# Products of an identity put ahead of the score products of a hybrid of four mixers

## The chip, the cores and the metric

The kernel runs on one core of one Trainium2 chip. The metric is the device time of one execution in microseconds. The engines are named as in the profile: PE is TensorE, DVE is VectorE, ACT is ScalarE, POOL is GpSimd, SP is SyncE.

## The reference

T = 256 positions, D = 1024, two layers, all in float32. Each layer projects h with w_in, gives a quarter of the result to each of four mixers, joins their outputs with w_out and normalises; then comes a feed-forward part, dense in layer 0, a mixture of 8 experts (top 2) in layer 1.

```python
for l in range(DEPTH):
    p = jnp.einsum('btd,dc->btc', h, w_in[l])
    pa, pb, pc, pd = _split(p, MIXER_COLS)
    ya = _hgrn2_mixer(pa, lb_all[l], hgrn_norm_g[l])
    yb = _gla_mixer(pb, gla_gate_w2[l], gla_gate_b[l], gla_norm_g[l])
    yc, v_first = _rwkv7_mixer(pc, v_first, v_mix, ...)
    yd = _retnet_mixer(pd, positions, log_gamma)
    mix = jnp.einsum('btc,cd->btd', jnp.concatenate([ya, yb, yc, yd], -1), w_out[l])
    h = _layer_norm(DN_ALPHA * h + mix, ln1_g[l], ln1_b[l])
    f = _swiglu(h, ...) if l % 2 == 0 else _moe(h, ...)
    h = _layer_norm(DN_ALPHA * h + f, ln2_g[l], ln2_b[l])
```

HGRN2 and GLA are the same recurrence, `out = q decay-weighted over the past (k, v)`: `scores = einsum('bhik,bhjk,bhijk->bhij', q, k, decay)`, `out = scores v + (q exp(cum)) state`. The mixer's output is normalised per head, multiplied by a gate and goes to w_out.

## The kernel before

Every float32 product of a weight matrix is done as three products of a rounded half H and a rest L (`wH` by ACT, line 133, `wL` by DVE, line 136; helper `mm` at 146 issues each matmul, `tr` at 149 each transposition). Their results are named `Pws_ps` and `Pas_ps` (projections by w_in, in two forms), `bank_acc` and `bank_r` (the products of w_out, whose left side is the mixers' outputs `YT`, and of the residual, `h` by `alphaI`). The four projections of a mixer are cut into jobs whose steps can be issued between other work: `between(n)` issues n steps of the pending jobs and then lets the body follow the last of them. The order on each engine is then set by the scheduler of the language from dependences and its own costs, so that it differs from the order of the code.

A layer's mixers run in the order RWKV, RetNet, HGRN2, GLA. RWKV walks over chunks (`Prw_po` is a chunk's output product, `rw_OC` the collected outputs); `head_norm` normalises per head, with the rsqrt (`hn_rs<-rs_ve,mhalf`) on POOL; the last step is the transposition of `rw_OC` into `Prw_ps14`, 16 pairs of 64x64 products. RetNet (`rt_o`) is normalised by the same helper.

HGRN2's scores (`hgrn_scores`) are formed for each half of the heads a and each of two heads s: decays by products with `c_hlR` (`Phs_ps`, `Phs_psd`), their exponentials `hg_E`, then nine small products over 64 partitions into the banks p1 and p2 (`Phs_p1p`), which the profile counts as 18. Two sets of them are 36. `Ppo_ps` are the output products by the scores (`lin_S`). GLA's (`gla_scores`) are alike: `gs_E`, two products per head into `Pgs_ps`, `Ppo_ps`; its gate products are `Pga_ps`. The normalised outputs of HGRN2 and GLA (`y_late`) are transposed late, inside w_out's loop (`LATE = (0, 2)`, `self.tails`, run from `down`), by four transpositions `Ppy_ps` each.

PSUM is in three pools: 3 banks for accumulation ("acc"), 2 for RWKV ("r") and 3 for the others ("o"). A helper `keep_warm(n)` multiplies the identity `eyeR` by itself (128 x 512 columns) n times into a bank of its own that nobody reads; it is used in a few places, among them between the two late transpositions of layer 0 (four products) and in the layer norms.

Of the kernel before, what the change touches and what calls it, by code (L numbers as in the profile page):

```python
# [44 lines left out]
TAIL, DT = 4, 4  # L45

WARM_NORM, WARM_LAST, WARM_ROUTE = 12, 4, 8

WARM_WAIT = 7

# [74 lines left out]
class Build:  # L125
# [88 lines left out]
    def keep_warm(self, n):  # L214

        b = self.acc()
        for _ in range(n):
            self.mm(b, self.eyeR, self.eyeR[:, None, :].to_broadcast([128, 4, 128]), True, True)


    def load(self, w, parts, cuts=1):
# [390 lines left out]
        self.rstd(rs, s2, eps, p)  # L612
        self.tt(o, o, rs[:, :, None].to_broadcast([128, n, 64]), OP.mult)

    def put_y(self, y, ct):

        ps = self.mx("Ppy_ps1")
        for a in range(2):
            for tt in range(2):
                self.tr(ps[:, a * 256 + tt * 128:a * 256 + tt * 128 + 128], y[:, tt, a * 128:(a + 1) * 128], self.ident)  # L620
        self.put_yt(ps, ct)
# [6 lines left out]
    def mixers(self, l):  # L628
        nc, I, c, p = self.nc, self.I, self.c, self.otp
        W = I["w_in"][l]  # L630
        self.mp, self.side, self.hp = self.rp, "r", HP
        ws = lambda c0: self.ws_steps(W, [(c0, c0 + 256)])
        as_ = lambda c0: self.as_steps(W, [(c0, c0 + 256)])
        self.jobs = []
# [92 lines left out]
    def gated_norm(self, o, g, G, ct):  # L727

        ng = self.bcast(self.t2([128, 64], n="gn_ng"), g)
        self.ts(ng, ng, 0.5, None, OP.mult, eng=self.nc.gpsimd)  # L730
        v = o.rearrange("p t (h v) -> p (t h) v", v=64)
        gv = G.rearrange("p t (h v) -> p (t h) v", v=64)
        self.tt(gv, gv, ng[:, None, :].to_broadcast([128, 8, 64]), OP.mult, self.nc.gpsimd)
        self.head_norm(v, 1e-6, False, "gn")
        if ct in LATE:
            o = self.lp.tile([128, 2, 256], F32, name="y_late")
        self.tt(o.rearrange("p t (h v) -> p (t h) v", v=64), v, gv, OP.mult)
        if ct in LATE:
            self.tails[ct] = lambda: self.put_y(o, ct)
        else:  # L740
            self.put_y(o, ct)

# [17 lines left out]
    def hgrn_scores(self, l, qT, kT, lf, V, o):  # L760
# [7 lines left out]
        for a in range(2):  # L768
# [31 lines left out]
            for s in range(2):  # L800
                r = slice(64 * s, 64 * s + 64)
                p1, p2 = self.mx("Phs_p1p21"), self.mx("Phs_p1p21")
                with self.between(FH):
                    for t in range(2):
                        self.mm(p1[:, t * 128:(t + 1) * 128], KD[r, t], QD[r, t], True, True)
                        self.mm(p1[:, 256 + t * 128:384 + t * 128], L16[r, t], L16[r, t], True, True)
                        self.mm(p2[:, t * 128:(t + 1) * 128], L32[r, t], L32[r, t], True, True)
                        self.mm(p2[0:64, 256 + t * 64:320 + t * 64], L64[r, t, 0:64], L64[r, t, 64:128], True, True)
                    self.mm(p2[:, 384:512], E[r, 0], E[r, 8], True, True)
# [12 lines left out]
    def gla_scores(self, l, qk, lf, V, o):  # L822
# [20 lines left out]
        for h in range(4):  # L843
            r = slice(32 * h, 32 * h + 32)
            ps = self.mx("Pgs_ps2")
            with self.between(FG):
                self.mm(ps[:, 0:256], E[r, 0, 0:128], E[r, 1, :], True, True)
                self.mm(ps[:, 256:384], E[r, 0, 128:256], E[r, 1, 128:256], True, True)
            d = ps.rearrange("p (t x) -> p t x", t=2)[:, :, 0:128]
# [127 lines left out]
    def rwkv(self, l, glr):  # L977
# [27 lines left out]
        self.stt(lwL, lw, 1.0, lwH.bitcast(F32), OP.add, OP.subtract)  # L1005

        A = self.t2([128, 2, T], n="rw_A")
        ps = self.mx("Prw_ps2").rearrange("p (a t) -> p a t", a=2)
        for a in range(2):
            self.mm(ps[:, a, :], a2[64:128, a * 128:(a + 1) * 128], lr[64:128, 0, :], True, True)  # L1010
        for a in range(2):
# [266 lines left out]
        ov = OC.rearrange("p c a v -> p (c a) v")  # L1278
        self.head_norm(ov, 64e-5, True, "rw")
        ps = self.mx("Prw_ps14")  # L1280
        for ch in range(4):
            for a in range(2):
                for s in range(2):
                    P, Q = slice(64 * s, 64 * s + 64), slice(64 - 64 * s, 128 - 64 * s)
                    self.mm(ps[P, a * 256 + ch * 64:a * 256 + ch * 64 + 64], OC[Q, ch, a, :], self.ident[Q, Q], True, True)
# [398 lines left out]
```

## Time and profile before

| what | us |
|---|---|
| median of three runs | 1094.89 (1093.45 to 1101.36) |
| profiled execution | 1099.03 |
| its span | 1097.2 |
| PE busy in it | 1040.8 |
| DVE busy | 789.8 |
| ACT busy | 616.8 |
| POOL busy | 60.5 |

The span is the time from the first instruction to the last; the execution's time lies a little above it. PEclk in a row is the clock that TensorE was granted, 1.00 being full speed (2.4 GHz), 0.50 the lower of its two levels (1.2 GHz). The mean granted clock of the profiled execution is 0.965.

In a row of the timeline, the first number is the start, the second the time that the group took, "x18" how many instructions it holds, and the bracket the idle time before it and who ended it.

### The profile page before, as it was taken

The page shows a single profiled execution, that of the slowest core. Times are in us where ns is not written, and L with a number is a line of the kernel's source. Part 1 is how long each engine was busy: PE and PEld are TensorE (multiplying, and loading weights), DVE is VectorE, ACT ScalarE, POOL GpSimd, SP SyncE. Part 2 cuts the span into 40 slices and gives each one's busy share as a digit, 9 for nine tenths or more (in the row PEclk, how much of TensorE's full clock was granted, in tenths as well). Part 3 has the DMA queues.
Part 4 walks back from the last instruction along what each step waited for, and adds up shares of the span by engine and source line. Part 5 has one row for each costly group of instructions (what it writes and reads, how often), then busy time and mean ns, then how long its engine had stood idle before and what let it go on. Part 6 is the DMA issues. An engine that isn't in the chain of part 4 may idle for free. (4 is left out here: it accounts for less than half of the span.)

```text
span 1097.2 us, 16969 instructions
## 1 busy us (share of the span) xinstructions
PE 1040.8 (95%) x6635; PEld 905.2 (83%) x6635; DVE 789.8 (72%) x1174; ACT 616.8 (56%) x872; POOL 60.5 (6%) x89
## 2 busy tenths in 40 slices
PE   7799989999999999899989989999999999999994
PEld 6788878789999788788877668888888888878883
DVE  4585674565556356675675578998999899989986
ACT  4634264435555342633264536787788678777862
POOL 2000021100000002000011210000000000010001
PEclk9899987999999999899988998999999999999997
DMA  9344144326666454244142095998899889979942
GB/s 299 99 119 128 57 154 155 116 78 192 193 192 228 157 192 156 87 115 131 65 164 78 12 366 191 359 381 302 313 348 362 307 306 364 357 269 328 365 179 80
DMA packets 142161, 228.83 MB, mean 209 GB/s; under 512 B 17604, under 2 KB 89848, under 8 KB 142072
## 3 DMA queue, kind: packets, MB, share of 16 engines
q1 hardware_dynamic: 135104, 219.76, 59.0%
q10 hardware_dynamic: 6968, 7.90, 2.2%
q8 instruction: 54, 0.88, 0.3%
q14 instruction: 35, 0.29, 0.1%
HBM read 224.50 MB, written 3.15 MB: 207 GB/s over the span
## 5 line engine op out<-in xcount | busy, mean ns | idle before, releaser
L136 DVE TENSOR_TENSOR wL<-raw,wH 128x1024 fp32r<-128x1024 f32 (+2 forms) x480 | 504.1, 1064 | 159.2 <-ACT wH L133 152.3
L133 ACT ACTIVATE wH<-raw 128x1024 fp32r<-128x1024 f32 (+2 forms) x481 | 441.9, 927 | 271.0 <-PE Pws_ps L146 95.8
L146 PE MATMUL Pws_ps<-XT,wH 128*128 128x256 f32 (+1 forms) x1248 | 233.2, 287 | 9.1 <-DVE rc_x L143 8.3
L146 PE MATMUL Pms_ps<-wH,e_X 128*128 128x512 f32 (+1 forms) x768 | 227.3, 374 | 0.0
L146 PEld LDWEIGHTS Pws_ps<-XT,wH 128*128 128x128 f32 (+1 forms) x1248 | 195.7, 191 | 12.8 <-DVE rc_x L143 9.2
L146 PE MATMUL Pws_ps<-XT,wL 128*128 128x256 f32 (+1 forms) x624 | 177.9, 286 | 0.0
L146 PEld LDWEIGHTS Pms_ps<-wH,e_X 128*128 128x128 f32 x768 | 142.3, 188 | 20.8
L146 PE MATMUL Pms_ps<-wL,e_X 128*128 128x512 f32 (+1 forms) x384 | 144.7, 377 | 1.0 <-DVE wL L136 1.0
L146 PEld LDWEIGHTS Pws_ps<-XT,wL 128*128 128x128 f32 (+1 forms) x624 | 119.3, 191 | 0.8 <-issue 0.3
L146 PE MATMUL bank_dn<-wH,e_aT 128*128 128x512 f32 x352 | 112.3, 396 | 0.6 <-DVE e_X L136 0.6
L146 PE MATMUL Pas_ps<-wH,XT 128*128 128x256 f32 x448 | 97.3, 305 | 4.6 <-ACT p_v L133 3.2
L146 PEld LDWEIGHTS Pas_ps<-wH,XT 128*128 128x128 f32 x448 | 76.8, 203 | 10.2 <-ACT p_v L133 4.5
L146 PEld LDWEIGHTS Pms_ps<-wL,e_X 128*128 128x128 f32 x384 | 72.2, 188 | 12.7 <-DVE wL L136 2.3
L146 PEld LDWEIGHTS bank_dn<-wH,e_aT 128*128 128x128 f32 x352 | 66.0, 188 | 16.7 <-DVE e_X L136 1.7
L146 PE MATMUL bank_dn<-wL,e_aT 128*128 128x512 f32 x176 | 69.4, 395 | 0.0
L146 PE MATMUL Pas_ps<-wL,XT 128*128 128x256 f32 x224 | 68.2, 305 | 0.5 <-DVE wL L136 0.5
L146 PEld LDWEIGHTS Pas_ps<-wL,XT 128*128 128x128 f32 x224 | 45.4, 203 | 3.1 <-DVE wL L136 1.8
L146 PEld LDWEIGHTS bank_dn<-wL,e_aT 128*128 128x128 f32 x176 | 33.1, 188 | 7.4
L146 PE MATMUL bank_acc<-wH,ffn_a 128*128 128x512 f32 x88 | 33.5, 394 | 0.0
L146 PE MATMUL bank_r<-wH,ffn_a 128*128 128x512 f32 x88 | 33.3, 392 | 0.0
L146 PE MATMUL bank_acc<-wH,YT 128*128 128x512 f32 x64 | 24.5, 416 | 1.2 <-ACT YT L133 1.2
L133 ACT ACT_TABLE_LOAD x19 | 24.4, 1283 | 1.6 <-PEq L1671 1.2
(386 smaller groups left out, 1223.8 us busy)
## 6 DMA issues: line engine op xcount, KB each, us to landing
raw<-in_moe_w_down SPq DMA_DIRECT2D x40, 1024.0 KB
raw<-in_moe_w_gate SPq DMA_DIRECT2D x32, 1024.0 KB
raw<-in_moe_w_up SPq DMA_DIRECT2D x32, 1024.0 KB
raw<-in_w_in SPq DMA_DIRECT2D x29, 1024.0 KB
raw<-in_moe_w_gate SPq DMA_DIRECT2D x16, 768.0 KB
raw<-in_moe_w_up SPq DMA_DIRECT2D x16, 768.0 KB
raw<-in_ffn_w_gate SPq DMA_DIRECT2D x11, 1024.0 KB
raw<-in_ffn_w_up SPq DMA_DIRECT2D x11, 1024.0 KB
```

Source lines behind the costliest of these rows:

```text
L133: return self.nc.scalar.activation(out=out, in_=in_, func=func, **k)
L136: return (eng or self.nc.vector).tensor_tensor(out=out, in0=a, in1=b, op=op)
L146: return self.nc.tensor.matmul(out=out, lhsT=lhsT, rhs=rhs, start=start, stop=stop)
```

## The change

A new method `fill(bank, n)` does what `keep_warm` does, but into a bank that it is given: the one that the real products right behind it in the code write. It is called in five places: 5 products ahead of RWKV's A product (layer 0 alone), 3 ahead of each of the eight score sets of HGRN2 (both layers, 24), 2 ahead of each head's scores of GLA (both layers, 16), 12 ahead of RWKV's last transposition (layer 1 alone) and 6 ahead of GLA's late transposition (layer 1 alone): 63 in all. Their values are overwritten.

```diff
+WARM_H, WARM_G, WARM_RW, WARM_LATE = 3, 2, 12, 6
...
+    def fill(self, bank, n):
+
+        for _ in range(n):
+            self.mm(bank, self.eyeR, self.eyeR[:, None, :].to_broadcast([128, 4, 128]), True, True)
...
-    def put_y(self, y, ct):
+    def put_y(self, y, ct, warm=0):
 
         ps = self.mx("Ppy_ps1")
+        self.fill(ps, warm)
...
+        self.later_layer = l > 0
...
-            self.tails[ct] = lambda: self.put_y(o, ct)
+            self.tails[ct] = lambda: self.put_y(o, ct, WARM_LATE if ct == LATE[-1] and self.later_layer else 0)
...
                 with self.between(FH):
+                    self.fill(p1, WARM_H)
                     for t in range(2):
...
             with self.between(FG):
+                self.fill(ps, WARM_G)
                 self.mm(ps[:, 0:256], E[r, 0, 0:128], E[r, 1, :], True, True)
...
-        ps = self.mx("Prw_ps2").rearrange("p (a t) -> p a t", a=2)
+        ps = self.mx("Prw_ps2")
+        self.fill(ps, 5 if l == 0 else 0)
+        ps = ps.rearrange("p (a t) -> p a t", a=2)
...
         ps = self.mx("Prw_ps14")
+        if l:
+            self.fill(ps, WARM_RW)
```

The helpers move by two lines, so `mm` is line 148 and `tr` line 151 in the changed kernel. Where the new products land is the scheduler's choice. Three places on PE follow, a row being instructions of one kind, with what they wait for.

HGRN2's scores of layer 0, first half of the heads: the end of the set s = 0 and the start of s = 1 on PE, before:

```order
L146 MATMUL Phs_p1p_1616<-hg_E 128x128
L146 MATMUL Phs_p1p_1616<-hg_E 64x64
L146 MATMUL Phs_p1p_1616<-hg_E 128x128 [waits Pool_49]
L146 MATMUL Phs_p1p_1683<-hg_E 128x128 [waits PE_49]
L146 MATMUL Phs_p1p_1683<-hg_E 128x128 x2
L146 MATMUL Phs_p1p_1684<-hg_E 128x128 [waits DVE_49,PE_49]
L146 MATMUL Phs_p1p_1684<-hg_E 64x64
```

and now:

```order
L148 MATMUL Phs_p1p_1621<-hg_E 128x128
L148 MATMUL Phs_p1p_1621<-hg_E 64x64
L148 MATMUL Phs_p1p_1621<-hg_E 128x128 [waits Pool_49]
L148 MATMUL Phs_p1p_1691<-eyeR 128x512 [waits PE_49]
L148 MATMUL Phs_p1p_1691<-eyeR 128x512 x2
L148 MATMUL Phs_p1p_1691<-hg_E 128x128 x2
L148 MATMUL Phs_p1p_1692<-hg_E 128x128 [waits DVE_49,PE_49]
L148 MATMUL Phs_p1p_1692<-hg_E 64x64
```

Three products on `eyeR` stand between the two sets, which had followed each other. Those of the set s = 0 stand six projection groups further ahead.

The end of RWKV in layer 1 on PE; `Pas_ps` are projections of a later mixer. Before, ahead of the transposition of `rw_OC` (41 more products of `Pas_ps` stand in a row above the first):

```order
L146 MATMUL Pas_ps_5885<-wH,XT 128x256 x2
L146 MATMUL Pas_ps_5885<-wL,XT 128x256
L146 MATMUL Pas_ps_5885<-wH,XT 128x256
L146 MATMUL Prw_ps_5683<-ident,rw_OC 64x64 [waits DVE_49,PE_49]
L146 MATMUL Prw_ps_5683<-ident,rw_OC 64x64 x15
L149 MATMUL Ppy_ps_5771<-ident,rt_o 128x128 [waits DVE_49]
L149 MATMUL Ppy_ps_5771<-ident,rt_o 128x128 x3
```

and now:

```order
L148 MATMUL Prw_po_5687<-rw_UV,rw_S 64x64 [waits DVE_49]
L148 MATMUL Prw_po_5687<-rw_UV,rw_S 64x64 x2
L148 MATMUL Prw_ps_5708<-eyeR 128x512 [waits PE_49]
L148 MATMUL Prw_ps_5708<-eyeR 128x512 x11
L148 MATMUL Prt_ps_5783<-p_v,rt_S_5759 128x64
L148 MATMUL Pas_ps_5640<-wH,XT 128x256
L148 MATMUL Pas_ps_5640<-wL,XT 128x256
...
L148 MATMUL Pas_ps_5641<-wH,XT 128x256
L148 MATMUL Prw_ps_5708<-ident,rw_OC 64x64 [waits DVE_49]
L148 MATMUL Prw_ps_5708<-ident,rw_OC 64x64 x15
L148 MATMUL Pas_ps_5922<-wH,XT 128x256 [waits Activation_49]
```

The 12 products stand behind the state products, and 25 products lie between them and the transposition. Seven of the 15 groups of three projection products that stood ahead of the transposition now stand behind it.

The two late transpositions of layer 1 on PE, HGRN2's first, GLA's second. Before:

```order
L146 MATMUL bank_r<-wH,YT 128x512
L149 MATMUL Ppy_ps_6486<-ident,y_late 128x128 [waits PE_49]
L149 MATMUL Ppy_ps_6486<-ident,y_late 128x128 x3
L146 MATMUL bank_acc<-wH,YT 128x512 [waits Activation_49]
L146 MATMUL bank_acc<-wL,YT 128x512
...
L146 MATMUL bank_r<-wH,YT 128x512
L146 MATMUL bank_r<-wL,YT 128x512
L149 MATMUL Ppy_ps_6503<-ident,y_late 128x128 [waits DVE_49]
L149 MATMUL Ppy_ps_6503<-ident,y_late 128x128 x3
L146 MATMUL bank_acc<-wH,YT 128x512 [waits DVE_49]
```

and now:

```order
L148 MATMUL bank_r<-wH,YT 128x512
L151 MATMUL Ppy_ps_6543<-ident,y_late 128x128 [waits PE_49]
L151 MATMUL Ppy_ps_6543<-ident,y_late 128x128 x3
L148 MATMUL Ppy_ps_6560<-eyeR 128x512 [waits PE_49]
L148 MATMUL Ppy_ps_6560<-eyeR 128x512 x5
L151 MATMUL Ppy_ps_6560<-ident,y_late 128x128 [waits DVE_49]
L151 MATMUL Ppy_ps_6560<-ident,y_late 128x128 x3
L148 MATMUL bank_acc<-wH,YT 128x512 [waits Activation_49]
L148 MATMUL bank_acc<-wL,YT 128x512
```

The new products stand ahead of the wait for GLA's `y_late`, and the eight w_out products that stood there now follow GLA's transposition.

## Rows read from the trace of the kernel before

**Rows 1.** the page: busy time and share of each engine, instructions

```profile
PE 1040.8 (95%) x6635; PEld 905.2 (83%) x6635; DVE 789.8 (72%) x1174; ACT 616.8 (56%) x872; POOL 60.5 (6%) x89
```

**Rows 2.** stretches: us; PE, PEld, DVE, ACT, POOL busy; PEclk; DMA share; GB/s

```profile
151.20:154.10 2.90, 2.90 (x23) 2.52 (x24) 1.77 (x6) 0.02 (x1) 0.00 (x0) 1.00 1.04 424
154.20:161.00 6.80, 6.80 (x26) 5.51 (x25) 3.31 (x7) 3.57 (x9) 0.46 (x1) 0.50 0.22 87
167.90:171.20 3.30, 3.30 (x17) 3.30 (x17) 0.37 (x2) 0.93 (x3) 0.00 (x0) 0.50 0.98 343
174.70:184.90 10.20, 10.20 (x47) 9.86 (x47) 4.05 (x5) 5.26 (x11) 3.62 (x3) 0.50 0.10 12
...
553.60:560.30 6.70, 6.20 (x52) 6.11 (x53) 3.92 (x8) 1.64 (x4) 0.00 (x0) 0.50 0.26 69
594.60:608.10 13.50, 13.50 (x51) 11.04 (x51) 3.31 (x7) 5.58 (x17) 3.81 (x4) 0.50 0.19 76
560.00:575.00 15.00, 15.00 (x118) 14.28 (x118) 12.87 (x22) 9.68 (x18) 0.00 (x0) 0.99 0.74 260
```

**Rows 3.** PE's timeline, layer 0, HGRN2's scores to GLA: start, us, instruction

```profile
151.21 6.33 PE L146 MATMUL Phs_p1p<-hg_E 64*128 64x128 f32 x36 [0.21 <-DVE hg_E L136]
...
168.27 0.63 PE L146 MATMUL Pas_ps<-wH,XT 128*128 128x256 f32 x2
...
168.91 0.63 PE L146 MATMUL Pas_ps<-wH,XT 128*128 128x256 f32 x2
...
175.75 3.51 PE L146 MATMUL Ppo_ps<-p_v,lin_S 128*128 128x64 f32 x16
...
185.19 0.40 PE L146 MATMUL Pas_ps<-wH,XT 128*128 128x256 f32 x2
...
185.55 0.40 PE L146 MATMUL Pas_ps<-wH,XT 128*128 128x256 f32 x2
```

**Rows 4.** timeline, end of RWKV: PE in both layers, layer 1's VectorE, GpSimd

```profile
138.85 1.15 PE L146 MATMUL Prw_ps<-ident,rw_OC 64*64 64x64 f32 x32 [1.36 <-DVE rw_OC L136]
...
554.10 1.97 PE L146 MATMUL Prw_ps<-ident,rw_OC 64*64 64x64 f32 x32 [4.45 <-DVE rw_OC L136]
...
544.83 0.69 DVE L605 TENSOR_REDUCE hn_s<-rt_o 128x8 f32<-128x512 f32 x1 [0.17 <-ACT rt_o L133]
...
546.22 0.69 DVE L136 TENSOR_TENSOR rt_o<-rt_o,hn_s 128x512 f32<-128x512 f32 x1
...
553.26 0.69 DVE L136 TENSOR_TENSOR rw_OC<-rw_OC,hn_rs 128x512 f32<-128x512 f32 x1 [0.93 <-POOL hn_rs L136]
...
549.94 3.29 POOL L136 TENSOR_TENSOR hn_rs<-rs_ve,mhalf 128x8 f32<-128x8 f32 x2 [60.11 <-DVE rs_ve L140]
```

**Rows 5.** PE's timeline, layer 1, HGRN2's scores and outputs, GLA's outputs

```profile
581.37 4.93 PE L146 MATMUL Phs_p1p<-hg_E 64*128 64x128 f32 x36
...
591.49 6.34 PE L146 MATMUL Phs_p1p<-hg_E 64*128 64x128 f32 x36 [0.87 <-DVE hg_E L136]
...
598.35 5.22 PE L146 MATMUL Ppo_ps<-p_v,lin_S 128*128 128x64 f32 x24
...
622.50 2.89 PE L146 MATMUL Ppo_ps<-p_v,lin_S 128*128 128x64 f32 x24
```

**Rows 6.** PE's timeline, layer 0: RWKV's A product, and existing products on eyeR

```profile
28.57 1.13 PE L146 MATMUL Prw_ps<-rc_x,rw_a 64*128 64x256 f32 x4 [1.32 <-DMA rw_a<-in_rwkv_a]
...
212.01 1.18 PE L146 MATMUL bank_acc<-eyeR 128*128 128x512 f32 x4
...
228.23 2.12 PE L146 MATMUL bank_acc<-eyeR 128*128 128x512 f32 x8
```

**Rows 7.** PE's timeline, layer 1: waits at GLA's scores and in out_proj

```profile
621.65 0.92 PE L146 MATMUL Pgs_ps<-gs_E 32*128 32x256 f32 x4 [0.55 <-ACT lin_S L133]
...
628.71 0.50 PE L146 MATMUL bank_acc<-wH,YT 128*128 128x512 f32 x1 [1.20 <-ACT YT L133]
...
633.08 0.66 PE L149 MATMUL Ppy_ps<-ident,y_late 128*128 128x128 f32 x4 [2.27 <-DVE y_late L136]
```

## The prediction

> **What bounds the kernel now.** I read the page first. TensorE (PE) is busy for 1040.8 of 1097.2 us [rows 1], so nearly every microsecond taken from PE's stream, or put into it, should show at the end unless it lies in one of PE's waits. The slices of granted clock say where else time hides: the profiled run's mean clock is 0.965. So the second view was the table by stretches, cut where the clock changes. It shows TensorE at 0.50, that is 1.2 GHz and not 2.4, from 154.2 to 161.0, 167.9 to 171.2, 174.7 to 184.9, 553.6 to 560.3 and 594.6 to 608.1 us, PE being busy all or nearly all of that time [rows 2]. The third view, PE's timeline, tells what PE did before: in layer 0 and again in layer 1 it ran HGRN2's scores, products of 64 partitions [rows 3, 5]; only ahead of 553.6 was it idle, 4.45 us, for rw_OC [rows 4]. I count 40.5 us at the low level in these five places; there are more elsewhere in the program that no new product touches, and I leave those as they are.
>
> The sum is made against the profiled run, 1099.03 us with a span of 1097.2; the median of the runs shown is 1094.89. I take the saving in microseconds from the one and subtract it from the other.
>
> **What a new product costs.** The kernel has the same product already: four of them take 1.18 us, eight take 2.12 [rows 6]. That is 0.30 and 0.27 us each with their start-up, and (2.12 - 1.18) / 4 = 0.24 for each further one. I take 0.24, since PE comes to them without a gap, and 0.30 as the upper bound. 63 of them are 15.1 us (up to 18.9) of PE time. What matters is how much falls into waits.
>
> **RWKV's A product, 5 products, 1.2 us: nothing.** They stand directly ahead of a product that waits 1.32 us for a DMA [rows 6]. If that load came sooner they would cost up to 1.2 us.
>
> **HGRN2 in layer 0, 12 products, 2.9 us paid.** PE is full there, so all of it is paid. What a full clock would give back, from rows at both levels: the 36 score products at 151.21 take 6.33 us, and the same 36 in layer 1 at full clock 4.93 [rows 3, 5], so 1.4. From their end at 157.5 to 161.0 there are 3.5 us of other products; a group of three projection products has a pitch of 0.64 us at the low level and 0.36 at the high one [rows 3], so 44% of such time is lost: 1.5. The stretch at 167.9 is such groups alone: 3.3 x 0.44 = 1.5. From 174.7 to 184.9, 16 output products in 3.51 us [rows 3], against 24 in 2.89 at full clock [rows 5]: 16 x (0.219 - 0.120) = 1.6; the other 6.7 us x 0.44 = 2.9. Together 8.9 us. The new products stand ahead of the scores: a score set no longer follows another directly, as the order shows. The first two stretches, 1.4 + 1.5 + 1.5 = 4.4, I count whole. Of the third, 4.5, I take two thirds, 3.0: it set in among the output products that follow the scores, and these get nothing put ahead of them. Bounds for it: 0 and 4.5. Net 7.4 - 2.9 = +4.5.
>
> **GLA in layer 0, 8 products, 1.9 us.** In the new order they replace seven residual and w_out products that stood ahead of the scores on gs_E; those go behind the outputs, and nothing else in front covers the wait for gs_E. I count the 1.9 and 0.5 for that wait: -2.4 (0 if the chain waits anyway, -3.5 if gs_E is late by more). Layer 0: +2.1.
>
> **RWKV's last transposition in layer 1, 12 products, 2.9 us.** The order says that they don't stand in the wait. They come straight behind the last state products; then come eight groups of Pas, then the transposition. Seven further groups (7 x 0.36 = 2.5 us) that stood ahead of it now stand behind it. So PE reaches the transposition about when it did, near 549.7 to 550.1. But VectorE's and GpSimd's order changes as well: the norm of RWKV now goes ahead of RetNet's. Before, two VectorE steps of RetNet went first (0.69 us each; I count 1.2, since such steps start before the last one's end) and RetNet's rsqrt too, one of the two that GpSimd does in 3.29 us, 1.65 [rows 4]. So rw_OC, ready at 553.95, comes some 2.9 us sooner, at 551.1. PE is then idle for about 1.0 to 1.4 us in place of 4.45, and layer 0 shows what follows such a gap: after 1.36 us of idling the transposition took 1.15 us and not 1.97 [rows 4]. Reckoned on: 551.1 + 1.15 + 2.5 for the moved groups = 554.75, to set against 554.10 + 1.97 = 556.0 before; then the 4.3 us to 560.3 at full clock are 2.4, against 4.3. PE stands at 557.15 in place of 560.3: +3.2. If the clock fell all the same: 551.1 + 1.97 + 7 x 0.64 = 557.6, and then 4.3: -1.6. I take +3.2, because the gap of layer 0 is the nearest row. What follows is PE without a gap from 560 to 575 [rows 2], so the gain is carried on.
>
> **HGRN2 in layer 1, 12 products, 2.9 us paid.** The low stretch is 13.5 us: scores 6.34 against 4.93, 1.4; 24 output products 5.22 against 2.89, 2.3 [rows 5]; the other 5.1 us x 0.44 = 2.2. Together 5.9. I count the scores whole and two thirds of the 4.5 behind them, 3.0, for the reason above. Net 4.4 - 2.9 = +1.5 (bounds -1.5 and +3.0).
>
> **GLA in layer 1 and its late transposition, 8 + 6 products, 3.4 us.** Here PE does wait: 0.55, 1.20 and 2.27 us [rows 7], 4.0 together, so they could be free. But the new order puts the eight w_out products of HGRN2's part, 8 x 0.24 = 1.9 us by the price of a product of the same shape, behind GLA's transposition, where they are paid; and it moves w_out products from ahead of GLA's scores to behind its outputs, which leaves the scores' chain bare and covers y_late's. I count -1.5, between 0 (all in waits) and -3.4 (none).
>
> **Sum.** Layer 0 +2.1; layer 1 +3.2 + 1.5 - 1.5 = +3.2; together 5.3 us saved: 1099.03 becomes 1093.7, the median 1089.6. Everything after (the MoE, where PE is busy throughout) starts that much sooner.
>
> **A rule that speaks against it.** At 154.2 the clock fell after a stretch of 2.90 us in which PE was busy for 2.90 [rows 2]. The Trainium skill (TensorE: Matmul & The Clock Gate, section "HAM oscillation — how this bites in real kernels") puts a re-throttled clock down to idle gaps of PE. By that rule HGRN2's scores, which leave no gap, would not be the cause and nothing ahead of them a cure. This case's trace does not agree at 154.2 and 594.6; it does at 553.6. The rule's outcome is the second rival below.
>
> **Rivals.** (1) Every one of the five low stretches goes, and the chain follows: the two thirds become whole (+1.5 + 1.5) and GLA's products lie in waits (+1.5, +2.4): 12.2 us, 1082.7. For it: no two score sets are left back to back in the order. Against it: HGRN2's outputs and GLA's gate products are still together. (2) Busy or not is what the clock goes by: HGRN2's products are paid and bring nothing, only RWKV's gap counts: -2.9 - 2.4 + 3.2 - 2.9 - 1.5 = -6.5, 1101.4, slower. It decides if 154.2 and 594.6 stay low in the new trace. Against it stand the rows just named; for it, the 36 scores at 581.37 ran through without a fall [rows 5], so scores alone don't always bring it. (3) The new order gives it back: the transposition in layer 1 doesn't do what the words say, since its products stand 25 products ahead of the wait, and the clock falls there too (-1.6 for +3.2), with the third stretch whole as before (-3.0 on the term): 5.3 - 4.8 - 3.0 = -2.5, about 1097.4; with one of the two, 1092.6 to 1094.4, no change.
>
> **How the numbers follow.** Forecast 0.57, within 1085 to 1093; (1) 0.20, with the low places elsewhere free to shift by two or three us, 1080 to 1085; (3) 0.16, 1093 to 1099; (2) 0.07, 1099 to 1104. The low end 1080 takes in (1); the high end 1099 takes in (3) and leaves (2). Within 1% of the median (1083.9 to 1105.8), which is about what a measurement of this kernel can tell from no change, lies all of the forecast and most of the rest; faster by more needs 11 us, the better half of (1) and a little luck elsewhere, 0.20; slower by more needs (2) with the new products at 0.30 each and RWKV's clock low, 0.05.
>
> **What would show it.** Right: the clock at 1.00 through HGRN2's first three score sets in both layers, 36 scores at some 4.9 us plus three new products; RWKV's transposition in layer 1 with an idle time of 1.0 to 1.4 us and 1.15 us long; RWKV's rsqrt first on GpSimd. Wrong: the low level still over the output products in both layers (then the gain is near 0), or an idle time of 2 us or more ahead of GLA's scores, or a new low stretch where the order moved products away. I would be wrong most easily by the low stretches that I left as they are: each costs 1.5 to 3 us and can come or go when the work ahead of it shifts.

## The result and the profile after

The changed kernel takes 1115.43 us in the median of four runs (1113.31 to 1116.32), the kernel before 1098.12 in four (1093.45 to 1103.11): a ratio of 1.0152, 95% interval 1.0116 to 1.0188. It is slower by some 17 us, outside my range on the slow side. The profiled execution after has a span of 1113.1 us, against 1097.2. This is the page's line of busy times after, to set beside [rows 1]:

```profile
PE 1053.8 (95%) x6698; PEld 912.3 (82%) x6698; DVE 790.9 (71%) x1174; ACT 615.7 (55%) x872; POOL 60.4 (5%) x89
```

The 63 products are there (6698 - 6635), and TensorE (PE) is busy 13.0 us longer, idle 2.9 us longer. The new products take 18.7 us of PE's time, from the start of each group to the next instruction's start, so the others got shorter by some 5.7. In this profile the clock did at HGRN2 what I had hoped, and the time did not follow. The view by stretches of the kernel after (us; PE, PEld, DVE, ACT, POOL busy; PEclk; DMA share; GB/s) has HGRN2 in layer 0 first and in layer 1 fourth, both at or near 1.00 where [rows 2] show 0.50, and new low stretches between and behind them, of which three are shown:

```profile
146.00:184.30 38.30, 33.97 (x243) 29.79 (x241) 22.98 (x48) 19.32 (x44) 7.99 (x12) 1.00 0.39 140
...
194.60:201.30 6.70, 6.70 (x18) 4.12 (x18) 1.27 (x4) 1.40 (x3) 1.63 (x1) 0.50 0.53 164
...
546.20:549.50 3.30, 3.30 (x13) 2.65 (x13) 2.13 (x5) 0.26 (x1) 0.00 (x0) 0.50 0.02 5
...
556.00:606.00 50.00, 43.33 (x307) 36.84 (x302) 30.76 (x63) 23.53 (x49) 5.49 (x9) 0.97 0.27 90
...
624.70:634.80 10.10, 10.10 (x36) 8.96 (x36) 2.96 (x5) 2.62 (x5) 2.26 (x3) 0.50 0.01 3
```

Over the whole span the mean granted clock rose only from 0.965 to 0.972. With two levels, 1.00 and 0.50, that is some 77 us at the low one before (2 x 0.035 x 1097.2) and 62 after (2 x 0.028 x 1113.1): 15 fewer, not the 40.5 of the five stretches, since others came in their place.

To find where the time went I cut both traces at the same instructions and compared lengths. The starts of the instructions come from PE's timeline, and the differences add up to the difference of the spans, 15.9 us (ln_dg is the layer norm behind w_out):

| from ... to | before, us | after, us | difference |
|---|---|---|---|
| start to RWKV's last transposition, layer 0 | 138.85 | 135.99 | -2.86 |
| to GLA's scores on gs_E, layer 0 | 57.61 | 53.62 | -3.99 |
| to the first product on ln_dg, layer 0 | 25.98 | 34.97 | +8.99 |
| to RWKV's last transposition, layer 1 | 331.66 | 331.10 | -0.56 |
| to GLA's gate (Pga), layer 1 | 49.40 | 50.19 | +0.79 |
| to GLA's outputs (Ppo), layer 1 | 19.00 | 18.64 | -0.36 |
| to the first product on ln_dg, layer 1 | 20.15 | 34.86 | +14.71 |
| to the end | 454.55 | 453.73 | -0.82 |

One piece, the end of GLA in layer 1, holds 14.7 us of it. In layer 0 the three pieces come to +2.1 us in this pair of traces; they vary from one trace to the next, and the runs below put a larger loss there. PE's timeline of the kernel after in the large piece (start, us, instruction; in brackets the idle time ahead and what ended it) answers to [rows 5] for the outputs and to [rows 7] for the transpositions; the last row here is the end of the piece after, and the row below it, alone, the end before:

```profile
624.51 5.28 PE L148 MATMUL Ppo_ps<-p_v,lin_S 128*128 128x64 f32 x24
...
640.55 0.60 PE L151 MATMUL Ppy_ps<-ident,y_late 128*128 128x128 f32 x4
640.91 1.62 PE L148 MATMUL Ppy_ps<-eyeR 128*128 128x512 f32 x6
642.37 0.60 PE L151 MATMUL Ppy_ps<-ident,y_late 128*128 128x128 f32 x4
...
652.45 0.80 PE L148 MATMUL bank_acc<-wH,YT 128*128 128x512 f32 x1 [4.11 <-ACT YT L135]
...
659.37 2.05 PE L148 MATMUL bank_o<-ln_dg,res 128*128 128x128 f32 x16 [1.70 <-DVE ln_dg L142]
```

```profile
642.65 2.05 PE L146 MATMUL bank_o<-ln_dg,res 128*128 128x128 f32 x16 [1.70 <-DVE ln_dg L140]
```

The outputs take 5.28 us and not 2.89, since they run at the low level. Between them and the first late transposition now stand 37 products of w_out; before there were 7. The views by stretches, of before and then of after, show what these take, 1.7 and 11.0 us, the latter in part at the low level:

```profile
625.20:626.91 1.71, 1.71 (x10) 1.35 (x9) 0.40 (x1) 1.02 (x2) 0.00 (x0) 1.00 0.08 19
```

```profile
629.55:640.55 11.00, 11.00 (x39) 8.80 (x39) 5.66 (x7) 4.08 (x5) 3.64 (x4) 0.76 0.24 70
```

And PE waits 4.11 us for YT, the transposed output of GLA that ScalarE (ACT) copies out of the bank. Why ACT was late is in its own timeline and that of the issues (ACTq and SPq are the queues' issue instructions; L1411 loads the router's weights e_rt, L1582 the MoE's). After:

```profile
636.74 0.92 SPq L1582 DMA_DIRECT2D raw<-in_moe_w_gate  x2
...
643.25 0.45 ACTq L1411 DMA_DIRECT2D e_rt<-in_moe_router  x1
...
651.66 0.26 ACT L135 ACTIVATE e_rHL<-e_rt 128x64 fp32r<-128x64 f32 x1 [9.36 <-DMA bc<-in_ln_b]
651.82 0.58 ACT L135 ACTIVATE YT<-Ppy_ps 128x512 fp32r<-128x512 f32 x1
```

Before:

```profile
628.88 0.46 ACTq L1396 DMA_DIRECT2D e_rt<-in_moe_router  x1
...
631.26 0.26 ACT L133 ACTIVATE e_rHL<-e_rt 128x64 fp32r<-128x64 f32 x1 [2.60 <-DMA e_rt<-in_moe_router]
...
633.18 1.07 SPq L1567 DMA_DIRECT2D raw<-in_moe_w_gate  x2
```

In ACT's order the copy of YT stands behind the split of e_rt (e_rHL), which waits for a small load. (The bracket after names bc, issued two places behind e_rt; in the traces of only_rw and before_moved, below, it names e_rt itself.) Before, that load was issued 4.3 us ahead of the MoE's first weights and ACT stood for 2.60 us; after, it was issued 6.5 us behind them, ACT stood for 9.36, the issues included, and GLA's transposition, done at 642.97, lay in its bank until 651.82.

### The profile page after: what moved, and what is told of

Its sections match the earlier page's. It is cut to its first block, busy times and chain, and to the rows that moved or that the text cites. A ratio compares the mean times of both kernels' runs of the same rounds, so it can differ in the third digit from the quotient of the medians.

```text
span 1113.1 us, 17095 instructions
## 1 busy us (share of the span) xinstructions
PE 1053.8 (95%) x6698; PEld 912.3 (82%) x6698; DVE 790.9 (71%) x1174; ACT 615.7 (55%) x872; POOL 60.4 (5%) x89
## 5 line engine op out<-in xcount | busy, mean ns | idle before, releaser
L148 PE MATMUL Pas_ps<-wH,XT 128*128 128x256 f32 x448 | 92.6, 295 | 5.2 <-ACT p_v L135 3.7
L148 PEld LDWEIGHTS Pas_ps<-wH,XT 128*128 128x128 f32 x448 | 73.4, 194 | 10.0 <-ACT p_v L135 5.0
L148 PE MATMUL Pas_ps<-wL,XT 128*128 128x256 f32 x224 | 65.7, 294 | 0.5 <-DVE wL L138 0.5
```

The lines of the kernel that those rows point to most:

```text
L148: return self.nc.tensor.matmul(out=out, lhsT=lhsT, rhs=rhs, start=start, stop=stop)
```

## The experiments

Two theories went in. **ORDER**: the new products take the places in which the scheduler had put w_out's, these go behind GLA's outputs, and the loss lies there, in products that no longer cover a wait and in ACT's queue. **PRICE**: the products are paid for, each at its own length on a full PE, and the loss is spread over their places. Each edit is shown against the kernel after where it is not said otherwise, with lines left out at "...". "A" is the group of 5 at RWKV's product on rw_a.

**1. HGRN2's 24 products alone** (only_h).

```diff
-WARM_H, WARM_G, WARM_RW, WARM_LATE = 3, 2, 12, 6
+WARM_H, WARM_G, WARM_RW, WARM_LATE = 3, 0, 0, 0
...
-        self.fill(ps, 5 if l == 0 else 0)
+        self.fill(ps, 0 if l == 0 else 0)
```

> The changed kernel with only HGRN2's 24 products; RWKV's, GLA's, A's and the late ones are left away. ORDER theory (the loss comes from the scheduler: it counts the new products' time in its plan and moves w_out and residual products from ahead of GLA's scores to behind GLA's outputs, 1.7 to 8.7 us of them in layer 1, 9.4 to 13.2 in layer 0, and small loads fall behind the MoE's): this kernel's own order leaves 2.2 us there in layer 1 and 10.8 in layer 0, so it should be 2 to 5 us faster than the kernel before. PRICE theory (PE is full, every new product costs its 0.24 us and nothing comes back): 24 x 0.24 = 5.8 us slower.

Measured: 1106.88 us, 1.0103 [1.0064, 1.0142]; some 11 us slower. Both theories missed: ORDER had a gain, PRICE the right sign and half the size. PE's timeline of this run, layer 0 and then layer 1:

```profile
191.53 0.47 PE L148 MATMUL Pgs_ps<-c_hlR,gs_lfH 128*128 128x128 f32 x1 [3.76 <-ACT gs_lfH L135]
...
599.57 4.74 PE L148 MATMUL Phs_p1p<-hg_E 64*128 64x128 f32 x18
```

In layer 1 the clock fell nevertheless: 18 scores take 4.74 us there, 2.72 at the full level, and the view by stretches has PE at 0.50 from 597.8 to 614.8 us. So these products by themselves bring no full clock, and in layer 0 a wait of 3.76 us opens ahead of GLA's decays. ORDER's cause is hardly at work here: 9 products of w_out stand between GLA's outputs and the first late transposition in layer 1, against 7 before, and the piece to ln_dg is 21.43 us long. The products' own time, 24 x 0.30 = 7.2 us, is the larger part of this loss.

**2. RWKV's 12 products alone** (only_rw): the same lines with `0, 0, 12, 0` and no A.

> The changed kernel with only the 12 products ahead of RWKV's last transposition in layer 1. ORDER theory: in this kernel's order 6.9 us of w_out products stand between GLA's outputs and the first late transposition of layer 1 (1.7 before), so it should be 6 to 10 us slower than before by itself, with an ACT stall ahead of the late transposed output as in the changed kernel. PRICE theory: 12 x 0.24 = 2.9 us slower; and if RWKV's wait pays for it, 3 us faster.

Measured: 1107.11 us, 1.0121 [1.0060, 1.0183]. The price of 12 products would be 0.3%; ORDER is nearer. The loss does not lie where the products stand but some 90 us later. ACT's timeline, and PE's, at the end of GLA in layer 1:

```profile
642.46 0.26 ACT L135 ACTIVATE e_rHL<-e_rt 128x64 fp32r<-128x64 f32 x1 [8.59 <-DMA e_rt<-in_moe_router]
```

```profile
643.25 0.79 PE L148 MATMUL bank_acc<-wH,YT 128*128 128x512 f32 x1 [3.54 <-ACT YT L135]
```

**3. GLA's 16 products alone** (only_g): `0, 2, 0, 0`, no A.

> The changed kernel with only GLA's 16 products. ORDER theory: in its order the w_out products behind GLA's outputs grow from 9.4 to 11.8 us in layer 0 and from 1.7 to 2.9 in layer 1, so 3 to 6 us slower than before. PRICE theory: 16 x 0.24 = 3.8 us slower. The two differ in where: ORDER has the time between GLA's outputs and the late transpositions.

Measured: 1108.94 us, 1.0119 [1.0064, 1.0173], more than either theory had. In its trace the piece from GLA's outputs to ln_dg in layer 1 is 27.44 us long (20.15 before), and ACT waits 8.54 us for e_rt. Three parts, each without the others, cost about the same, 1.0 to 1.2%, and all together 1.5%: they do not add up. One likely reason, which I did not test: e_rt's late load is paid once, and RWKV's products bring it about by themselves, as GLA's do. It isn't that each pushes back the same w_out products: between GLA's outputs and the first late transposition of layer 1 stand 37 of them after the change, 29 in only_rw, 12 in only_g, 9 in only_h.

**4. The change with e_rt's split on GpSimd** (after_rhl), so that ACT has no load to stand for ahead of YT.

```diff
-        self.split(self.rHL[:, :, 0:NE], self.rHL[:, :, 32:40], rt)
+        rH = self.rHL[:, :, 0:NE]
+        nc.gpsimd.tensor_copy(rH, rt)
+        self.tt(self.rHL[:, :, 32:40], rt, rH.bitcast(F32), OP.subtract, nc.gpsimd)
```

> The changed kernel whole; only the split of the router's weights (e_rHL) is done by GpSimd in place of ACT and VectorE, so that ACT doesn't wait for that small load. PE's order is the same as in the changed kernel. If the wait of ACT's queue for the load (9.36 us in the changed kernel's trace, with the late transposed YT behind it) is on the path: 4 to 8 us faster than the changed kernel, and PE's idle time of 4.11 us ahead of w_out's last products gone. If it isn't (PRICE theory, or the order of PE alone): within 1 us of the changed kernel.

Measured: 1109.52 us, 1.0168 [1.0092, 1.0244], with one of four runs at 1121.5; by time alone it tells nothing. Its trace does: ACT copies YT directly behind the issue of the last load, and PE's wait of 4.11 us is gone; the piece to ln_dg is 27.47 us, 7.4 shorter. PE is idle 4.1 us less in it, and 6.8 us of it are at the low level and not 13.7.

```profile
643.06 0.42 ACTq L407 DMA_DIRECT2D bc<-in_ln_b  x1
643.52 0.60 ACT L135 ACTIVATE YT<-Ppy_ps 128x512 fp32r<-128x512 f32 x1 [2.60 <-issue]
```

**5. A's five products alone** (only_a): `0, 0, 0, 0`, A kept.

> The changed kernel with only the 5 products ahead of RWKV's A product in layer 0. WAIT theory (these five lie in a wait for a DMA and let the order behind them run sooner): the trace of the changed kernel is 2.9 us ahead at RWKV's transposition in layer 0, and of the runs with single parts none without these products is, so 2 to 4 us faster than the kernel before. PRICE theory (each new product is paid): 5 x 0.24 = 1.2 us slower.

Measured: 1094.04 us, 0.9962 [0.9937, 0.9986]. This beats the kernel before by 0.4%. PE's timeline of this run answers to [rows 6]:

```profile
26.51 1.51 PE L148 MATMUL Prw_ps<-eyeR 128*128 128x512 f32 x5
...
40.27 0.50 PE L148 MATMUL Pws_ps<-XT,wH 128*128 128x256 f32 x2 [3.07 <-DVE rc_x L145]
```

The products lie in the wait for the load, as forecast, and RWKV's last transposition comes at 135.51 in place of 138.85. It came at 135.3 to 136.2 in five traces with A at 512 columns, and at 138.8 to 141.3 in eight without.

**6. No new product, w_out moved** (before_moved): the kernel before, in which 36 of layer 1's w_out products, those of three of the eight blocks of its inner dimension (7, 4 and 5), are held until after GLA's last output product.

```diff
+MOVED = lambda s, nk, k: not s.general and nk == KT and s.proj_layer == 1 and k in (7, 4, 5)
...
+                    self.po_last = self.mm(ps[:, v], S(2, h), V[:, 0, v], False, True).ins
-                    self.mm(ps[:, v], S(2, h), V[:, 0, v], False, True)
...
+        self.proj_layer = l
...
+                    with (self.tc.issue_after(self.po_last) if MOVED(self, nk, k0 + i // 2) else nullcontext()):
-                    for tt in range(2):
-                        mms(tt, k0 + i // 2, i % 2, H, L)
+                        for tt in range(2):
+                            mms(tt, k0 + i // 2, i % 2, H, L)
```

> The kernel before, with no new product; only in layer 1 three of the four first k-groups of w_out's products (36 products, 8.5 us by the order, 1.7 before) are queued behind GLA's last output product, as they stand in the changed kernel. ORDER theory (what costs most in layer 1 is that these products leave the GLA chain bare, come after it, and push ACT's small loads behind the MoE's): 8 to 12 us slower than the kernel before with no product added, a low clock behind GLA's outputs, and PE idle ahead of GLA's scores. PRICE theory (the loss is the new products' own time on a full PE): within 2 us of the kernel before.

Measured: 1107.25 us, 1.0083 [1.0048, 1.0118]; 7 us slower by the medians, 9 by the ratio, with not one product more. This decides for ORDER in layer 1: from RWKV's transposition to ln_dg there the trace takes 102.8 us, the change 103.7, and four traces whose layer 1 has neither 88.6 to 91.5. Its PE timeline shows what the products had covered: GLA's scores now wait 2.25 us, and the outputs come no sooner after RWKV's transposition than before (69.6 us, 68.4 before), though almost 7 us of w_out have been taken out ahead of them. The outputs run at the low level, as after the change, and ACT and PE wait as there. The rows are PE's timeline, the view by stretches of the piece to ln_dg, and ACT's timeline.

```profile
612.39 1.67 PE L148 MATMUL Pgs_ps<-gs_E 32*128 32x256 f32 x12 [2.25 <-DVE gs_E L138]
...
616.45 5.38 PE L148 MATMUL Ppo_ps<-p_v,lin_S 128*128 128x64 f32 x24
...
642.03 0.80 PE L148 MATMUL bank_acc<-wH,YT 128*128 128x512 f32 x1 [3.48 <-ACT YT L135]
```

```profile
616.45:649.70 33.25, 27.53 (x108) 22.19 (x107) 12.30 (x20) 10.81 (x15) 4.43 (x6) 0.78 0.53 182
```

```profile
641.24 0.26 ACT L135 ACTIVATE e_rHL<-e_rt 128x64 fp32r<-128x64 f32 x1 [8.53 <-DMA e_rt<-in_moe_router]
```

**7. The change with w_out brought forward again** (after_hip): a higher priority for two groups of its products.

```diff
+HIP = lambda nk, k0: nk == KT and k0 in (6, 4)
...
+                    with (self.tc.high_priority() if HIP(nk, k0) else nullcontext()):
```

> The changed kernel with all 63 products; w_out's products of the first four k-groups are given a higher priority with the scheduler, so that some come back among GLA's steps: 5.5 us of them in place of 8.7 stand between GLA's outputs and the first late transposition of layer 1 (1.7 before). ORDER theory: 2 to 5 us faster than the changed kernel (1110 to 1113 beside its 1115). PRICE theory: within 1 us of it.

Measured: 1114.61 us, 1.0127 [1.0087, 1.0166], not to be told from the change itself. The views by stretches of this run show why: the piece from GLA's outputs to ln_dg shrinks to 28.31 us (34.86 after), but the one ahead of it, from the gate to the outputs, grows to 24.99 (18.64).

```profile
609.30:634.29 24.99, 22.46 (x114) 17.81 (x113) 11.89 (x21) 11.60 (x25) 4.29 (x4) 0.93 0.25 86
...
634.29:662.60 28.31, 23.17 (x100) 17.58 (x100) 12.80 (x21) 11.64 (x16) 4.41 (x6) 0.88 0.66 225
```

I read it so that the room there is now held by the new products, and bringing the others back only makes PE's stream longer in the other piece; no run tests that by itself.

**8. The 63 products with 8 columns in place of 512** (after_thin).

```diff
-            self.mm(bank, self.eyeR, self.eyeR[:, None, :].to_broadcast([128, 4, 128]), True, True)
+            self.mm(bank[:, 0:8], self.eyeR, self.eyeR[:, 0:8], True, True)
```

> The changed kernel with all 63 products at 8 columns in place of 512, so that they take hardly any time on PE; the scheduler counts them as cheap, and its order has w_out's products of layer 1 nearly as before (2.2 us behind GLA's outputs, 1.7 before). ORDER and PRICE theories alike: near the kernel before, within 4 us. What it tells is the clock: if the time of the low level in HGRN2's and GLA's stretch of layer 0 is 20 us again as before (3.4 in the changed kernel, 13.7 with its twin), then it is the work of the full products that keeps the clock up; if it is low here as well, the clock there is chance.

Measured: 1111.06 us, 1.0099 [1.0063, 1.0135]; a miss for both. A thin product isn't free. RWKV's twelve take 2.72 us by the row below, and all 63 some 9 us, against 18.7 for the full ones; w_out is pushed back hardly at all in layer 1 (the piece to ln_dg is 21.74 us). In the trace's sum PE is busy 15.0 us longer than before and idle 4.3 us less. The 6 us of busy time beyond the products go with the clock, whose mean is 0.961 here, against 0.965 before and 0.972 after the change: more of layer 0's start and of HGRN2 in layer 1 is at the low level than after the change. Why it is, I did not settle.

```profile
546.36 2.72 PE L148 MATMUL Prw_ps<-eyeR 128*128 128x8 f32 x12
```

**9 and 10. The change in layer 0 alone, A with it** (l0_only), **and in layer 1 alone** (l1_only). The new products are made to depend on the layer, in layer 0 for the first:

```diff
-                    self.fill(p1, WARM_H)
+                    self.fill(p1, WARM_H if l == 0 else 0)
...
-                self.fill(ps, WARM_G)
+                self.fill(ps, WARM_G if l == 0 else 0)
...
```

> The changed kernel with the new products of layer 0 alone (5 + 12 + 8); layer 1 is in the order of the kernel before. ORDER theory (most of the loss is w_out's products of layer 1 leaving their place): 0 to 5 us slower than the kernel before, of which the traces of layer 0 say +5.0 from RWKV's transposition to the layer norm and -2.9 ahead of it. PRICE theory (each product is paid wherever it stands): 25 of 63, 25 x 0.27 = 6.8 us slower.

> The changed kernel with the new products of layer 1 alone (12 + 12 + 8 + 6); layer 0 is in the order of the kernel before. ORDER theory: 11 to 16 us slower than the kernel before, all of it between RWKV's last transposition and the layer norm behind w_out, the larger part behind GLA's outputs. PRICE theory: 38 x 0.27 = 10.3 us slower, with the idle time of PE not grown.

Measured: l0_only 1101.47 us, 1.0035 [1.0012, 1.0058]; l1_only 1108.87 us, 1.0114 [1.0039, 1.0189]. The two add up to 1.49%, the whole is 1.52%, though the interval of the second is wide. Beside the 1098.3 us measured with them, layer 1 costs 10.6 by the medians and 12.5 by the ratio, layer 0 with A 3.2 and 3.8. Since A alone gains 0.38%, HGRN2's and GLA's products in layer 0 cost some 0.73%, 8 us. The traces agree: from RWKV's transposition to ln_dg in layer 0 the four with all these products take 88.6 to 89.0 us, the seven with none of them 76.4 to 83.6.

**11. Moved w_out as in 6, and e_rt's split on GpSimd as in 4** (moved_rhl), **and 12. that split in the kernel before** (before_rhl), as its control.

> The kernel before with the 36 products of w_out moved behind GLA's outputs, as in the run with that edit alone (0.83% slower than before), and the split of the router's weights taken from ACT to GpSimd. If ACT's wait for that small load, with the late YT behind it, is a part of what the move costs: 3 to 6 us faster than the move alone, so 0.3 to 0.5% slower than before, PE's idle time ahead of w_out's last products gone. If only PE's order matters: 0.8% slower as with the move alone.

> The kernel before with that split taken from ACT to GpSimd and nothing else, a control: in the trace of before the load has landed 2.6 us after the issue and the late YT waits for PE, not for ACT's queue. So within 2 us of the kernel before under either theory.

Measured: moved_rhl 1102.33 us, 1.0040 [1.0011, 1.0069]; before_rhl 1099.56 us, 1.0008 [0.9982, 1.0034], no change. With ACT's standing for e_rt taken away, about half of the cost of the move is gone (0.83% becomes 0.40%; the intervals overlap, but the traces say the same, 27.20 us to ln_dg by the row below in place of 33.25). What the other half is I read from the trace alone: PE is idle 5.47 us between GLA's gate and its outputs, 0.85 before, and at the low level over the outputs.

```profile
616.73:643.93 27.20, 24.63 (x108) 20.49 (x107) 12.00 (x19) 10.91 (x14) 4.99 (x8) 0.86 0.41 134
```

**Same order, different clock.** Seven traces have the order of the kernel before in layer 0, so they compare its clock without a further run. These are views by stretches from RWKV's last transposition to GLA's scores, of before, l1_only, before_moved and only_a in turn.

```profile
138.85:196.46 57.61, 54.99 (x344) 47.81 (x344) 35.12 (x70) 31.29 (x66) 10.64 (x13) 0.82 0.41 143
```

```profile
139.99:196.07 56.08, 53.50 (x344) 46.86 (x344) 35.05 (x70) 31.28 (x66) 10.63 (x13) 0.85 0.42 148
```

```profile
138.85:190.06 51.21, 47.57 (x345) 40.75 (x345) 35.80 (x70) 31.07 (x66) 10.31 (x13) 0.97 0.44 162
```

```profile
135.51:185.96 50.45, 46.36 (x344) 39.46 (x345) 35.73 (x70) 31.06 (x66) 10.32 (x13) 1.00 0.46 164
```

The seven traces with this order have 0 to 20.5 us of it at the low level, and 50.5 to 57.6 us in all. The low stretches on which I put 8.9 us were a draw of one execution. The new products did not end them either: with all of them, in the same PE order as after, after_rhl has 13.7 us of the piece at the low level, 10.3 of them together from 151.1 to 161.4, among HGRN2's scores.

```profile
135.84:193.24 57.40, 51.81 (x349) 45.40 (x349) 33.35 (x67) 29.81 (x62) 9.73 (x13) 0.88 0.41 144
```

In layer 1 it is otherwise: the piece from the transposition to GLA's gate was 49.4 to 50.0 us long in six traces without new products there, with 15.3 to 15.9 us at the low level each time.

## Why the prediction was wrong

I forecast 5.3 us of gain and the kernel lost 17. In PE's sum, the new products took 18.7 us (15.1 forecast), the others got shorter by 5.7, and PE's idle time, which was to shrink at RWKV and at A, grew by 2.9. The sum doesn't say where; the runs do.

The step that failed first and most is "GLA in layer 1 and its late transposition": I counted -1.5 there, "between 0 (all in waits) and -3.4 (none)"; the piece grew by 14.7 us in the trace, and the change in layer 1 alone was timed at 1.14%, some 11 to 12 us. I had read from the order that w_out's products go behind GLA's outputs and wrote that this "covers y_late's" wait, as if covering one wait at no cost in another.

Three things were missing, as the runs showed. The w_out products cost nothing where they had stood, in waits for gs_E and lin_S that the rest of the chain needs anyway, and are paid in full behind the outputs: 30 of them at 0.23 us, 7 us, and 9.3 as it was, in part at the low level; before_moved shows it without any new product. The waits at that place don't shrink, as GLA's outputs come after a chain over ACT and VectorE (DVE). And I had asked of moved PE products only what PE does; with them moved ACT's order, where the small load for e_rt is issued and its split stands ahead of YT. That gave the 9.36 us above, about half of the move's cost by moved_rhl against before_moved. The low clock over the outputs, from 624.7 to 634.8, appears in before_moved and moved_rhl too, but it is no fixed part: l1_only, with layer 1 in the same PE order as after, ran them at the full level in 2.89 us, and only_h, which moved hardly any w_out product, had them low. I had named "a new low stretch where the order moved products away" as a sign of being wrong, and given it no price.

**HGRN2 in layer 0**, +4.5 in my sum, is the second. The mechanism looked confirmed in the profile after, 1.00 through the scores, where [rows 2] have 0.50. It isn't: without a single new product there, only_a was at 1.00 for the whole piece, and with all twelve after_rhl was low among the scores. What the low level costs I had about right, 57.61 - 50.45 = 7.2 us between before and only_a; that the products would end it was wrong, and so their price stays. In the new order a full clock right ahead of GLA's decays is also worth less than the sum of the shorter instructions. PE's timeline of the kernel after, at GLA's decays:

```profile
184.48 0.48 PE L148 MATMUL Pgs_ps<-c_hlR,gs_lfH 128*128 128x128 f32 x1 [3.86 <-ACT gs_lfH L135]
```

In l0_only, where 10.2 us of the piece were at the low level and not 3.4, that product started at 184.49 without a wait. The chain over VectorE and ACT sets this place; the clock gained just ahead of it goes into the wait. (Over the scores themselves the low level did cost time: after_rhl's piece is 57.40 us, its wait at the decays 3.88.) So the piece is 53.62 us after and 53.83 in l0_only, 3.2 to 3.4 longer than the old order at full clock, about what HGRN2's 12 products take (3.54).

**GLA in layer 0** I had at -2.4; from the scores on, the piece grew by 9.0 us, and by 5.4 to 5.6 in after_rhl and after_hip, where it was at the full clock. Eight products of the residual and five of w_out that had stood ahead of the scores are paid behind the outputs (the eight take 3.1 us in after_rhl), and I had given them no price: the same fault as in layer 1. For a bare wait I had counted 0.5 us; at gs_E it is 0.34 after and 1.12 in l0_only. The wait of 3.86 us above is ahead of the decays; that the moved products would have covered it isn't shown, since l0_only has none in the same order and only_h 3.76 with the residual's products still in front. The rest after the change goes with the low level from 194.6 to 201.3 us.

**RWKV's transposition in layer 1** I had at +3.2. The part that I could read from layer 0 held: 1.15 us long, with 1.47 us idle ahead, against [rows 4]. What did not was rw_OC's arrival "some 2.9 us sooner, at 551.1". The timelines of PE, ACT, VectorE and GpSimd after:

```profile
546.84 4.29 PE L148 MATMUL Prw_ps<-eyeR 128*128 128x512 f32 x12
550.96 0.33 PE L148 MATMUL Prt_ps<-p_v,rt_S 128*128 128x64 f32 x2
...
555.68 1.15 PE L148 MATMUL Prw_ps<-ident,rw_OC 64*64 64x64 f32 x32 [1.47 <-DVE rw_OC L138]
...
551.33 0.39 ACT L135 ACTIVATE rt_o<-Prt_ps 128x256 f32<-128x256 f32 x1 [1.45 <-PE Prt_ps L148]
...
551.75 0.69 DVE L612 TENSOR_REDUCE hn_s<-rt_o 128x8 f32<-128x512 f32 x1 [1.15 <-ACT rt_o L135]
...
554.93 0.69 DVE L138 TENSOR_TENSOR rw_OC<-rw_OC,hn_rs 128x512 f32<-128x512 f32 x1 [1.56 <-POOL hn_rs L138]
...
552.81 2.09 POOL L138 TENSOR_TENSOR hn_rs<-rs_ve,mhalf 128x8 f32<-128x8 f32 x1 [60.35 <-DVE rs_ve L142]
```

The twelve products fell into a low stretch and took 4.29 us, not 2.9. RetNet's last two output products stand right behind them, ACT copies those, and VectorE does a RetNet reduction on them before it hands RWKV's rs_ve to GpSimd: I had RetNet's steps behind RWKV's, and one was still ahead. GpSimd does do RWKV's rsqrt first, but at 552.81. The transposition came 0.56 us sooner, reckoned from layer 0's ln_dg (331.10 us, where the six traces without new products in layer 1 have 330.9 to 331.8), and its gain of 0.8 in length is all there is beside that. Nor was it "carried on", as I had it: behind the transposition PE now waits 2.00 us for p_v and more after that. In only_rw, with no other new product, PE's idle time from there to GLA's gate is 7.1 us, against 2.7 before, while the wait ahead of the transposition had fallen by 3.0. The cost of these products further on was what mattered, 1.2% by only_rw.

**HGRN2 in layer 1**, +1.5: the piece from the transposition to the gate became 0.8 us longer, the shorter transposition included. Here a gain in clock is real, at least for all the products of layer 1 together: with them 3.4 us of the piece are low and not 15.3 or more, in l1_only as after the change. PE is busy for 43.52 us in place of 46.73 in spite of 3.3 us of new products, but idle for 6.7 in place of 2.7: ahead of the scores PE waits 1.24 us for ACT's hg_E and 0.91 for VectorE's, and at a projection 2.00 for p_v. The idle time goes with RWKV's products more than with HGRN2's: it is 7.1 us in only_rw and 2.5 in only_h. I had counted no wait.

**A** I counted at nothing; it gained 0.4%. It lies in the wait, as said, and the gain comes behind it: PE's wait for rc_x is 3.07 us in place of 4.52, which I hadn't looked for; the rest of the 3.3 us I did not trace. **The price** was 0.30 us a product in the mean, my upper bound, not 0.24: 18.7 us for the 63. At the full level a further product did follow 0.23 us after the last; small groups pay their start-up more often, and some ten ran at the low level, 0.43 us apart.

Of the rivals, (1) is out: the low stretches went and the time rose. (2) is out by its own sign, since 154.2 and 594.6 did not stay low; but for layer 0 that sign was a draw too, and that HGRN2's products there are paid and bring nothing, as it had it, is what the runs show. The rule of the Trainium skill (TensorE: Matmul & The Clock Gate, section "HAM oscillation — how this bites in real kernels") that stands beside it, a clock lost to idle gaps, is not borne out here, and no run isolates it: in layer 0, in the same order, only_a was at 1.00 with 4.09 us of idle time, before at 0.82 with 2.62. (3) named the true kind of cause, that the new order gives the gain back, but looked for it at RWKV and priced it at 8 us at most.

So the runs put the loss in two places. In layer 1 the move of w_out alone, with e_rt's late load, makes the stretch from RWKV's transposition to ln_dg as long as the whole change does (102.8 and 103.7 us). The change's 26 new products in that stretch are about paid for by the clock, 17 us of it being low and not 43 as in before_moved. In layer 0 the clock brings nothing back: from RWKV's transposition to ln_dg 10 to 17 us are low with the new products, 0 to 20.5 without. The 8 us lost there are an estimated 20 x 0.30 = 6.0 for the products themselves and a rest that goes with the moved ones. No run separates price from order in layer 0.

Three things stay open. HGRN2's products alone cost 1.0%, of which 24 x 0.30 = 7.2 us is price and the rest only in part the low stretch in layer 1. Why the clock was lower with the thin products is not explained. And the six products of the late transposition were not run by themselves.

## What to carry to other kernels

Products without use that a scheduler is given to place are work like any other to it: they take the gaps in which it had put real products, and these turn up later, where they may be on the path (36 of them, moved with nothing added, cost 0.83% here); so list what leaves a wait along with what enters it, and follow the other engines' orders and DMA issues at the place where it lands. Don't price a low clock from one profile: compare the same stretch, in the same order, in several executions, and ask whether another engine's chain sets its end anyway. A group of such products in a wait for a load, with nothing displaced, can pay by itself.

## What the runs showed of the hardware

The clock's low stretches differ from one trace to the next at the same order of PE's instructions: 0 to 20.5 us of one piece of layer 0 in seven traces. Products of 8 columns follow each other at 0.11 us on PE at the full level (after_thin) and those of 512 at 0.23 (after), so 64 times fewer columns save only half. And a small load (e_rt, 0.45 us to issue), split on ACT, kept ACT standing for 6.5 to 9.4 us in the six traces that issued it behind the MoE's first weight loads, and for 2.6 in the five that issued it ahead of them. In only_h it was issued 0.55 us ahead of them (2.61), in before_moved 0.55 us behind (8.53). Why the load is slower there, no run shows.
